# Load slots and look-ahead in a two-layer decoder trunk: eight slots for seven, modulation tiles three ahead for two

## The chip, the core and the metric

The kernel runs on one core of a Trainium2 chip. Its engines are TensorE (PE, with its weight loads PEld in rows of their own), VectorE (DVE), ScalarE (ACT), GpSimd (POOL) and SyncE (SP), which here only issues transfers. Each engine works through its own list of instructions in order. The metric is the device time of one execution in microseconds; lower is better. It is taken as the median of several runs.

## The reference: what is computed

Two decoder layers over one sequence of 256 tokens, width 2048, all in float32. Layer 0 mixes tokens by gated linear attention (GLA), layer 1 by softmax attention with forget gates (FoX); each is followed by a gated MLP of inner width 5632 with a causal convolution of width 3. Every sub-layer is modulated by a vector made from the condition `c`:

```python
cond = jax.nn.silu(c)
for i in range(DEPTH):
    mod = (cond @ w_mod[i] + b_mod[i])[:, None, :]
    sh_m, sc_m, g_m, sh_f, sc_f, g_f = jnp.split(mod, 6, axis=-1)
    h = rmsnorm(x, norm_mix[i]) * (1.0 + sc_m) + sh_m
    y = gla_mixer(h, ...) if i % N_MIXERS == 0 else fox_mixer(h, ...)
    x = x + (1.0 + g_m) * y
    h = rmsnorm(x, norm_ffn[i]) * (1.0 + sc_f) + sh_f
    x = x + (1.0 + g_f) * conv_ffn(h, ffn_w_up[i], ...)
return rmsnorm(x, norm_final)
```

So there are two kinds of large reads. The weights of the mixers and of the MLPs go to TensorE against 256 tokens. The modulation matrix `w_mod` (2 x 2048 x 12288 numbers) meets a single vector, and its product is needed at the start or the end of each sub-layer.

## The kernel before

**Tiles.** Weights come as tiles of 128 x 1024 numbers (4 KB in each of 128 partitions, 512 KB in all). A list made ahead of time, `plan`, holds them in the order of use. The full float32 precision is reached by splitting: ScalarE rounds a weight tile `w` to a high part `wh` (line 117), VectorE computes the rest `wl` (line 121), and TensorE runs three products for each piece (lines 612 to 614; 648 to 650 where the activations are stationary). One weight tile makes 24 matmuls of 128x128 against 256 columns. `wh` and `wl` have `AHEAD + 1` = 4 buffers each, so splits run at most some three tiles ahead of TensorE.

**Modulation.** `w_mod` is read as tiles `wm` of the same size. After the start VectorE takes them: for each one a multiply-add `acc = wm * c + acc` over 128x1024 (line 271, the first of a sum line 269). 16 such tiles make 1024 columns; then `acc` is summed over partitions (lines 283, 284, 300, 304) and written into `mod`. A sub-layer's `h` reads `mod`, and so do the residuals.

**The ring.** `w` and `wm` tiles share one pool of buffers, `ring`, with RING = 7 slots. A transfer into a slot waits until the tile that held it has been read for the last time: a `w` by its split on line 121, a `wm` by its multiply-add. All these transfers stand in SP's one queue, in a fixed order; one that waits for a slot holds up those behind it.

**Who asks when.** `next_w` hands out the next weight tile and calls `split_to`, which issues loads for up to `RING - 1` = 6 tiles ahead of the one to split next. After each tile's matmuls `tick` runs: it calls `prefetch(PEND)`, which issues modulation loads until PEND = 2 of them are pending, and then `steps`, which takes as many multiply-adds from the pending ones (`bg_step`) as `pace["bg"]` says. `set_pace(n)` spreads the queued modulation tiles over n ticks: 32 tiles over 44 ticks in the first GLA stage, over 43 in the first stage of the MLP of layer 0. `drain_bg` takes all that are left, at the ends of such stages.

**What sets the order.** The functions record instructions in the order of the program; a scheduler then orders each engine's list by a timeline of its own, in which it also hands out the slots. `tc.issue_after` keeps a multiply-add behind the latest split. So a change of slots or of load order can shift other instructions by some places.

Of the kernel before, what the change touches and what calls it, by code (L numbers as in the profile page):

```python
# [28 lines left out]
GH = 4  # L29
FH = 16  # L30
SECT = {"sh_m": 0, "sc_m": 1, "g_m": 2, "sh_f": 3, "sc_f": 4, "g_f": 5}
RING = 7
AHEAD = 3
DIRECT = 4
XAFTER = 1
# [2 lines left out]
BACK = 1  # L38
STAGE = 3
FREE = 0  # L40
PEND = 2
BLOCKS = (8, 8)
FIRST = (6, 0)
SLOW = 0.0
# [26 lines left out]
def kernel(  # L71
# [10 lines left out]
    const = ctx.enter_context(tc.tile_pool(name="const", bufs=1))  # L82
    ring = ctx.enter_context(tc.tile_pool(name="ring", bufs=RING))
    big = ctx.enter_context(tc.tile_pool(name="big", bufs=NBIG))
# [15 lines left out]
    def ringt(shape, s="w"):  # L100
        return ring.tile(shape, F32, tag="w", name=nm(s))
# [10 lines left out]
    def split_w(src, moving, after=None):  # L112
        n_ = src.shape[-1]
        o1, o2 = (0, 0) if moving else HELD
        hi = tmp.tile([P, WCOLS], F32R, tag="wh", bufs=AHEAD + 1, name=nm("wh"))[:, o1:o1 + n_]
        lo = tmp.tile([P, WCOLS], F32R, tag="wl", bufs=AHEAD + 1, name=nm("wl"))[:, o2:o2 + n_]
        nc.scalar.copy(out=hi, in_=src)  # L117
        with ExitStack() as es:
            if after is not None:
                es.enter_context(tc.issue_after(after))  # L120
            order["v"] = nc.vector.tensor_tensor(out=lo, in0=src, in1=hi.bitcast(F32), op=ALU.subtract).ins  # L121
        return hi, lo
# [106 lines left out]
    def after_startup(on=True):  # L229
        es = ExitStack()  # L230
        if on and startup["left"] > 0 and len(startup["loads"]) >= BACK:
            startup["left"] -= 1
            es.enter_context(tc.issue_after(startup["loads"][-BACK]))
        return es
# [115 lines left out]
    def prefetch(depth):  # L350
        while bg and len(pending) < depth:
            load, f = bg.popleft()
            load()
            pending.append(f)
# [6 lines left out]
    def flush_resting(all_=False):  # L361

        for r in resting:
            r[0] -= 1
        while resting and (all_ or resting[0][0] <= 0):
            resting.popleft()[1]()

    def tick():
        prefetch(PEND)
        flush_resting()  # L370
        with ExitStack() as es:
            for key in ORDERED:
                if order[key] is not None and fetched["use"] > FREE:
                    es.enter_context(tc.issue_after(order[key]))
            steps()
# [185 lines left out]
    def next_w(kt, cols, hold=None):  # L561
        i = fetched["use"]
        assert plan[i][1] == kt and plan[i][3] == tuple(cols), (plan[i][1:], kt, cols)
        fetched["use"] += 1
        run, look = AHEAD if hold is None else hold, RING - 1
        if i < STAGE:
            run, look = min(run, STAGE - i), 1
        split_to(min(i + 1 + run, len(plan)), look)
        return splits.popleft()

    def split_to(end, look=RING - 1):
        while fetched["split"] < end:
            while fetched["load"] < min(fetched["split"] + look, len(plan)):
                w_, kt_, nk_, cols_, mov_ = plan[fetched["load"]]
                fetched["load"] += 1
                wt = ringt([P, 1024])
                o = 0
                for c0, cn in cols_:
                    if nk_ == 1:
                        with after_startup():  # L580
                            nc.sync.dma_start(out=wt[:, o:o + cn], in_=w_[kt_ * P:(kt_ + 1) * P, c0:c0 + cn])
                        o += cn
                    else:
                        nc.sync.dma_start(out=wt[:, :nk_ * cn].rearrange("p (k r) -> p k r", r=cn),
                                          in_=w_[kt_ * P:(kt_ + nk_) * P, c0:c0 + cn]
                                          .rearrange("(k p) r -> p k r", p=P))
                        nc.vector.memset(wt[:, nk_ * cn:nk_ * cn + P - cn], 0.0)
                        o = nk_ * cn + P - cn
                raws.append((wt[:, :o], mov_))
            with ExitStack() as es:  # L590
                after = None
                if gate["n"] > 0:

                    gate["n"] -= 1
                    es.enter_context(tc.issue_after(gate["early"] if gate["n"] > 0 else gate["late"][0]))
                    after = gate["late"][1]
                splits.append(split_w(*raws.popleft(), after))
            fetched["split"] += 1
# [4 lines left out]
    def stream_a(kts, cols, rhs, done=None):  # L603
# [12 lines left out]
        for k in kts:  # L616
            rh, rl = rhs(k)
            tail = done is not None and k in kts[-TAIL:]
            wh, wl = next_w(k, cols, kts[-1] - k + 1 if tail else None)
            if tail:  # L620
                held.append((k, wh, wl, rh, rl))
                continue
            for m in range(8):
                mms(m, k, wh, wl, rh, rl)
            tick()
        if done is not None:
            split_to(min(fetched["use"] + 1, len(plan)))
            if len(deferred) > 1:
                deferred.pop(0)()
            for m in range(8):  # L630
                for args in held:
                    mms(m, *args)
                if m % 2 == 1:
                    done(m // 2, ps)
        return ps

    def stream_b(kts, c0, lhs):
        ps = [b.rearrange("p j t -> p (j t)") for b in banks()]
        for k in kts:
            lh, ll = lhs(k)  # L640
            wh, wl = next_w(k, [(c0, 1024)])
            first, last = k == kts[0], k == kts[-1]
            for tt in range(TT):
                ts_ = slice(tt * P, (tt + 1) * P)
                for hf in range(2):
                    hs_ = slice(hf * 512, (hf + 1) * 512)
                    o = ps[tt * 2 + hf]
                    nc.tensor.matmul(o, lh[:, ts_], wh[:, hs_], start=first, stop=False)  # L648
                    nc.tensor.matmul(o, ll[:, ts_], wh[:, hs_], start=False, stop=False)  # L649
                    nc.tensor.matmul(o, lh[:, ts_], wl[:, hs_], start=False, stop=last)  # L650
            tick()
        return ps

    def narrow(kts, c0, nn, lhs):
        pa = misc()
        lhs(kts[0])
        nh, nl = next_w(kts[0], [(c0, nn)])
        for k in kts:
            lh, ll = lhs(k)
            cs = slice((k - kts[0]) * nn, (k - kts[0]) * nn + P)  # L660
            first, last = k == kts[0], k == kts[-1]
            nc.tensor.matmul(pa[:, :T], nh[:, cs], lh, start=first, stop=False)
            nc.tensor.matmul(pa[:, :T], nh[:, cs], ll, start=False, stop=False)
            nc.tensor.matmul(pa[:, :T], nl[:, cs], lh, start=False, stop=last)
        return pa
# [669 lines left out]
```

## Time and profile before

| | |
|---|---|
| median of 3 runs | 2452.31 us (2449.97 to 2458.36) |
| the profiled execution | 2452.57 us |
| its span, first to last instruction | 2450.8 us |
| TensorE / VectorE / ScalarE / GpSimd busy | 98% / 79% / 51% / 1% |
| read from HBM | 633.14 MB, 259 GB/s over the span |
| mean granted TensorE clock | 0.987 of full speed |

The span and the busy times come from the first part of the profile. An engine's busy time counts its own instructions; a matmul's end is modelled and overlaps the next one's start, so a busy TensorE can still be held up for parts of a microsecond between two starts, and only a longer hold shows as idle time. A row of the view by stretches of time gives for one stretch its length and, for each engine, the busy time with the number of instructions, then the granted clock, the busy share of the DMA engines and their rate.

### The profile page before, as it was taken

How to read it: one execution, taken by the hardware profiler on the slowest of the kernel's cores; microseconds unless marked ns; L12 is line 12 of the kernel's file. 1: busy time of each engine (PE TensorE's matmuls, PEld its weight loads, DVE VectorE, ACT ScalarE, POOL GpSimd, SP SyncE). 2: the span in 40 equal slices, each digit the busy share in tenths (PEclk: the TensorE clock that was granted, in tenths of full speed). 3: DMA queues.
4: the chain of work that ended last, by engine and by line, in shares of the span. 5: the costliest groups of instructions: out<-in, count | busy, mean ns of one | idle time of the engine just before them, and what ended most of it. 6: DMA issues, size and time to landing. Idle time of an engine off the chain costs nothing.

```text
span 2450.8 us, 46953 instructions
## 1 busy us (share of the span) xinstructions
PE 2401.6 (98%) x19147; PEld 2313.5 (94%) x19150; DVE 1926.7 (79%) x2587; ACT 1254.9 (51%) x1700; POOL 16.5 (1%) x35
## 2 busy tenths in 40 slices
PE   6999999999999999999999999999999999999998
PEld 6998899899999999999988888999999999999998
DVE  7777989887789999987587898887876777777544
ACT  2456555444655555543454545554655555555433
POOL 0000000000000000000000000000000000000000
PEclk7999999899999999999999999999999999999999
DMA  9897878798668888999589887687677777756553
GB/s 371 281 314 239 301 260 313 277 315 313 201 192 273 304 290 307 308 336 320 182 287 311 302 291 235 222 292 250 220 236 233 233 235 237 230 194 220 192 190 112
DMA packets 184309, 638.32 MB, mean 260 GB/s; under 512 B 23961, under 2 KB 24971, under 8 KB 183708
## 3 DMA queue, kind: packets, MB, share of 16 engines
q1 hardware_dynamic: 183128, 634.12, 76.8%
q8 instruction: 150, 2.46, 0.4%
q10 hardware_dynamic: 964, 1.20, 0.1%
q14 instruction: 67, 0.55, 0.1%
HBM read 633.14 MB, written 2.10 MB: 259 GB/s over the span
## 4 chain that ended last, share of the span: by engine, by line
PE 88%; DVE 5%; DMA 5%; issue 1%; ACT 0%; SPq 0%; DVEq 0%; ACTq 0%
PE pa L614 23%; PE pa L613 23%; PE pa L612 23%; PE pa L650 5%; PE pa L649 5%; PE pa L648 5%; DMA wm<-in_w_mod_dram 4%; DVE wl L121 2%; DVE acc L271 1%; PE pm L483 0%; PE pt L293 0%; PE pm L852 0%; DMA w<-in_gla_w_in_dram 0%; PE pm L1063 0%; PE pm L874 0%
## 5 line engine op out<-in xcount | busy, mean ns | idle before, releaser
L117 ACT CAST wh<-w 128x1024 fp32r<-128x1024 f32 x819 | 855.9, 1048 | 985.4 <-PE pa L613 686.2
L121 DVE TENSOR_TENSOR wl<-w,wh 128x1024 fp32r<-128x1024 f32 x819 | 993.4, 1219 | 315.5 <-ACT wh L117 311.3
L613 PE MATMUL pa<-h,wh 128*128 128x256 f32 x3584 | 992.3, 278 | 2.3 <-DVE h L530 2.3
L614 PE MATMUL pa<-h,wl 128*128 128x256 f32 x3584 | 990.8, 278 | 3.5 <-DVE wl L121 3.5
L612 PE MATMUL pa<-h,wh 128*128 128x256 f32 x3584 | 990.6, 278 | 3.3 <-ACT h L528 1.8
L614 PEld LDWEIGHTS pa<-h,wl 128*128 128x128 f32 x3584 | 673.1, 188 | 7.1 <-DVE wl L121 4.5
L613 PEld LDWEIGHTS pa<-h,wh 128*128 128x128 f32 x3584 | 675.5, 189 | 3.3 <-DVE h L530 3.1
L612 PEld LDWEIGHTS pa<-h,wh 128*128 128x128 f32 x3584 | 673.6, 189 | 4.4 <-ACT h L528 2.2
L271 DVE SCALAR_TENSOR_TENSOR acc<-wm,cT,acc 128x1024 f32<-128x1024 f32 x352 | 451.9, 1284 | 131.0 <-DMA wm<-in_w_mod_dram 129.4
L613 PE MATMUL pa<-op,wh 128*128 128x256 f32 x1920 | 527.9, 277 | 0.4 <-DVE op L546 0.4
L612 PE MATMUL pa<-op,wh 128*128 128x256 f32 x1920 | 527.2, 277 | 0.0
L614 PE MATMUL pa<-op,wl 128*128 128x256 f32 x1920 | 523.6, 277 | 0.4 <-DVE wl L121 0.4
L613 PEld LDWEIGHTS pa<-op,wh 128*128 128x128 f32 x1920 | 360.5, 188 | 0.6 <-DVE op L546 0.6
L612 PEld LDWEIGHTS pa<-op,wh 128*128 128x128 f32 x1920 | 359.8, 188 | 0.0
L614 PEld LDWEIGHTS pa<-op,wl 128*128 128x128 f32 x1920 | 357.3, 188 | 0.8 <-DVE wl L121 0.6
L649 PE MATMUL pa<-wh,h 128*128 128x512 f32 x512 | 200.1, 392 | 0.0
L648 PE MATMUL pa<-wh,h 128*128 128x512 f32 x512 | 198.7, 392 | 0.0
L650 PE MATMUL pa<-wl,h 128*128 128x512 f32 x512 | 194.3, 393 | 0.0
L1115 ACT ACTIVATE y<-u,cw 128x256 f32<-128x256 f32 x176 | 101.8, 599 | 30.9 <-DVE act L1131 28.6
L648 PEld LDWEIGHTS pa<-wh,h 128*128 128x128 f32 x512 | 96.2, 188 | 19.3 <-issue 0.2
L650 PEld LDWEIGHTS pa<-wl,h 128*128 128x128 f32 x512 | 95.9, 188 | 19.5 <-DVE wl L121 0.3
L649 PEld LDWEIGHTS pa<-wh,h 128*128 128x128 f32 x512 | 96.2, 188 | 19.1
(258 smaller groups left out, 1350.6 us busy)
## 6 DMA issues: line engine op xcount, KB each, us to landing
wm<-in_w_mod_dram SPq DMA_DIRECT2D x352, 512.0 KB, 5.2
w<-in_ffn_w_up_dram SPq DMA_DIRECT2D x320, 512.0 KB, 4.5
w<-in_ffn_w_down_dram SPq DMA_DIRECT2D x176, 512.0 KB, 4.5
w<-in_fox_w_in_dram SPq DMA_DIRECT2D x128, 512.0 KB, 5.0
w<-in_gla_w_in_dram SPq DMA_DIRECT2D x96, 512.0 KB, 5.1
wm<-in_w_mod_dram SPq DMA_DIRECT2D x16, 1024.0 KB, 12.3
w<-in_gla_w_out_dram SPq DMA_DIRECT2D x32, 512.0 KB, 6.0
w<-in_ffn_w_up_dram SPq DMA_DIRECT2D x64, 256.0 KB, 4.1
```

Of the source, the lines that this page charges most:

```text
L117: nc.scalar.copy(out=hi, in_=src)
L121: order["v"] = nc.vector.tensor_tensor(out=lo, in0=src, in1=hi.bitcast(F32), op=ALU.subtract).ins
L271: nc.vector.scalar_tensor_tensor(out=st["a"], in0=wt[:, j, :], scalar=col, in1=st["a"], op0=ALU.mult, op1=ALU.add)
L612: nc.tensor.matmul(o, wh[:, ms], rh, start=(first and m % 2 == 0), stop=False, skip_group_check=True)
L613: nc.tensor.matmul(o, wh[:, ms], rl, start=False, stop=False, skip_group_check=True)
L614: nc.tensor.matmul(o, wl[:, ms], rh, start=False, stop=last, skip_group_check=True)
L648: nc.tensor.matmul(o, lh[:, ts_], wh[:, hs_], start=first, stop=False)
L649: nc.tensor.matmul(o, ll[:, ts_], wh[:, hs_], start=False, stop=False)
L650: nc.tensor.matmul(o, lh[:, ts_], wl[:, hs_], start=False, stop=last)
L1115: nc.scalar.activation(y, u, AF.Identity, scale=cw[:, l * 3 + 2, r:r + 1], bias=cw[:, 6 + l, r:r + 1])
```

## The change

The ring gets an eighth slot. The look-ahead of the weights, which was tied to the number of slots, gets a constant of its own with the value that it had, 6. The number of modulation tiles that `tick` keeps asked for goes from 2 to 3. The number of multiply-adds per tick, and the tick in which each is recorded, stay as they were.

```diff
-RING = 7
+RING = 8
+LOOK = 6
...
-PEND = 2
+PEND = 3
...
-        run, look = AHEAD if hold is None else hold, RING - 1
+        run, look = AHEAD if hold is None else hold, LOOK
...
-    def split_to(end, look=RING - 1):
+    def split_to(end, look=LOOK):
```

One line is added above, so line 250 of before is line 251 of the changed kernel, and so on.

SP's queue at the end of the first stage of the MLP of layer 0 (`w` are weight tiles, `wm` modulation tiles; numbers only tell tiles apart), before:

```order
L250 DMA wm_6345<-in_w_mod_dram 128x1024
L581 DMA w_6348<-in_ffn_w_up_dram 128x1024
L250 DMA wm_6378<-in_w_mod_dram 128x1024
L581 DMA w_6381<-in_ffn_w_up_dram 128x1024
L250 DMA wm_6411<-in_w_mod_dram 128x1024
L581 DMA w_6422<-in_ffn_w_up_dram 128x1024
L581 DMA w_6453<-in_ffn_w_up_dram 128x1024
L250 DMA wm_6483<-in_w_mod_dram 128x1024
L581 DMA w_6486<-in_ffn_w_up_dram 128x1024
```

The same place of SP's queue now:

```order
L251 DMA wm_6347<-in_w_mod_dram 128x1024
L582 DMA w_6350<-in_ffn_w_up_dram 128x1024
L251 DMA wm_6380<-in_w_mod_dram 128x1024
L582 DMA w_6383<-in_ffn_w_up_dram 128x1024
L251 DMA wm_6413<-in_w_mod_dram 128x1024
L582 DMA w_6424<-in_ffn_w_up_dram 128x1024
L582 DMA w_6455<-in_ffn_w_up_dram 128x1024
L582 DMA w_6486<-in_ffn_w_up_dram 128x1024
```

The two lists end at the same weight tile, `w_6486`. In the first the last modulation tile of the stage (`wm_6483`) stands directly ahead of it; in the second the last one (`wm_6413`) stands three weight tiles ahead of it. The weights keep their order, each with one modulation tile more ahead of it.

VectorE's list where the second GLA stage adds up `q` (the four `L725` rows read the TensorE banks `pa`; `L693` belongs to the gate), before:

```order
L725 TENSOR_TENSOR q_713<-q_713,pa_2007 128x512
L271 SCALAR_TENSOR_TENSOR acc_2078<-wm_2226,cT,acc_2078 128x1024
L725 TENSOR_TENSOR q_713<-q_713,pa_2008 128x512
L121 TENSOR_TENSOR wl_2289<-w_2083,wh_2288 128x1024
L725 TENSOR_TENSOR q_713<-q_713,pa_2009 128x512
L725 TENSOR_TENSOR q_713<-q_713,pa_2010 128x512
```

And now:

```order
L726 TENSOR_TENSOR q_715<-q_715,pa_2007 128x512
L726 TENSOR_TENSOR q_715<-q_715,pa_2008 128x512
L122 TENSOR_TENSOR wl_2291<-w_2085,wh_2290 128x1024
L272 SCALAR_TENSOR_TENSOR acc_2080<-wm_2228,cT,acc_2080 128x1024
L726 TENSOR_TENSOR q_715<-q_715,pa_2009 128x512
L726 TENSOR_TENSOR q_715<-q_715,pa_2010 128x512
```

The multiply-add that stood between the first and the second sum of `q` now stands behind the second one and behind the split that follows it.

## The prediction

> **What bounds the kernel now.** First the busy times, then the chain that ended last:
>
> ```profile
> span 2450.8 us, 46953 instructions
> PE 2401.6 (98%) x19147; PEld 2313.5 (94%) x19150; DVE 1926.7 (79%) x2587; ACT 1254.9 (51%) x1700; POOL 16.5 (1%) x35
> PE 88%; DVE 5%; DMA 5%; issue 1%; ACT 0%; SPq 0%; DVEq 0%; ACTq 0%
> ```
>
> TensorE is the bound: it is busy for 2401.6 of 2450.8 us, so 49.2 us of idle time are all that any change of loads can take away, the start and the end included. The change touches no matmul. The question is which of the 49.2 us lie in the middle and who causes them. The view by stretches of 50 us gives the place (columns: length, busy time of PE, PEld, DVE, ACT, POOL, granted clock, DMA share, GB/s):
>
> ```profile
> 0.00:50.00 50.00, 36.62 (x168) 34.37 (x169) 33.93 (x58) 11.81 (x20) 1.18 (x9) 0.82 0.98 385
> ...
> 150.00:200.00 50.00, 47.21 (x382) 45.69 (x381) 35.36 (x33) 22.37 (x32) 0.00 (x0) 0.99 0.89 302
> 200.00:250.00 50.00, 48.39 (x375) 44.77 (x374) 37.00 (x50) 38.93 (x57) 0.00 (x0) 0.97 0.72 232
> 450.00:500.00 50.00, 45.65 (x335) 42.48 (x335) 41.24 (x68) 21.70 (x29) 0.00 (x0) 0.86 0.70 248
> 500.00:550.00 50.00, 48.79 (x430) 48.59 (x429) 38.85 (x36) 24.87 (x31) 0.00 (x0) 1.00 0.92 323
> 550.00:600.00 50.00, 48.22 (x420) 47.66 (x419) 35.40 (x35) 22.66 (x26) 0.00 (x0) 1.00 0.87 305
> 600.00:650.00 50.00, 47.70 (x417) 47.31 (x417) 38.32 (x57) 27.85 (x37) 0.00 (x0) 1.00 0.73 239
> 650.00:700.00 50.00, 50.00 (x443) 50.00 (x443) 40.76 (x59) 28.64 (x39) 0.00 (x0) 1.00 0.61 194
> 850.00:900.00 50.00, 49.55 (x437) 49.35 (x436) 45.12 (x61) 28.76 (x39) 0.00 (x0) 1.00 0.90 307
> 900.00:950.00 50.00, 49.46 (x433) 49.20 (x433) 47.71 (x64) 28.70 (x42) 0.00 (x0) 1.00 0.90 303
> 950.00:1000.00 50.00, 49.11 (x429) 48.57 (x428) 49.41 (x71) 31.01 (x44) 0.00 (x0) 1.00 0.88 298
> 1000.00:1050.00 50.00, 49.64 (x437) 49.41 (x436) 48.43 (x58) 26.25 (x32) 0.00 (x0) 1.00 0.90 318
> ```
>
> Unhindered, TensorE starts 443 matmuls in 50 us (650 to 700), 0.113 us each, so a weight tile of 24 takes 2.71 us. The other rows fall short of it by 0.4 to 4.4 us. Who is late there tell the lists of waits, of the whole span and of VectorE alone in two stretches (80 to 200, then 500 to 615 us; columns: us in total, times, longest):
>
> ```profile
> ACT wh L117 <- PE pa L613: 686.2, 458, 4.0
> DVE acc L271 <- DMA wm<-in_w_mod_dram: 129.4, 111, 3.2
> ...
> DVE acc L271 <- DMA wm<-in_w_mod_dram: 34.6, 22, 3.2
> ...
> DVE acc L271 <- DMA wm<-in_w_mod_dram: 27.8, 21, 2.6
> ...
> SPq L581 <- DVE wl L121: 958.9, 485, 16.6
> SPq L250 <- DVE wl L121: 304.9, 245, 13.1
> ```
>
> Three things are to be seen. ScalarE's cast of a weight waits mostly for TensorE to free a buffer: weights are there early. VectorE's multiply-add waits for the modulation tile to land, 129.4 us in all. And SP cannot issue a load until a split or a multiply-add has freed a slot. So modulation tiles are late, and weight tiles wait in slots; while VectorE waits, the splits queued behind the multiply-add wait too, and so do the slots that they would free. Mostly the four split buffers cover it. Three places where they do not, in the chain and in VectorE's timeline (start, duration):
>
> ```profile
> 190.66 6.08 DMA wm<-in_w_mod_dram
> 196.84 1.29 DVE acc L271
> 198.18 1.09 PE pm L304 x8
> ...
> 238.95 1.28 DVE L271 SCALAR_TENSOR_TENSOR acc<-wm,cT,acc 128x1024 f32<-128x1024 f32 x1 [1.81 <-DMA wm<-in_w_mod_dram]
> 240.15 0.68 DVE L725 TENSOR_TENSOR q<-q,pa 128x512 f32<-128x512 f32 x1
> ...
> 589.93 6.03 DMA wm<-in_w_mod_dram
> 596.28 0.98 issue
> 597.26 1.50 DVE wl L121 x2
> ```
>
> At 190.66 the last modulation tile of the first GLA stage is issued, lands 6.08 us later, and TensorE's transposes of the sum start only at 198.18. At 238.95 a multiply-add that waited 1.81 us holds up the sum of `q`, whose banks TensorE needs. At 589.93 the late tile holds up a split.
>
> **The change, part by part.** The eighth slot and PEND = 3 belong together. The order of SP's queue shows what they do: every modulation load moves one modulation step forward, and every weight keeps its place with one tile more ahead of it, for which there is one slot more. So a weight waits for the same release as before, and a modulation tile for one that comes a step earlier. A step is 2.71 us over the tiles per tick: 44/32 x 2.71 = 3.73 us in the first GLA stage, 43/32 x 2.71 = 3.64 us in the first MLP stage. The longest waits there are 3.2 and 2.6 us. Each is shorter than a step, so, transfers taking no longer than now, all of them go. What is late next at these places is TensorE itself.
>
> Transfers do take longer when more are under way. At full pace the first MLP stage wants 1 + 32/43 = 1.744 tiles of 0.524 MB in 2.71 us, 338 GB/s. What the DMA engines can do shows the start, 385 GB/s (row above), and this stretch:
>
> ```profile
> 415.00:462.00 47.00, 47.00 (x417) 47.00 (x416) 43.77 (x49) 20.47 (x37) 0.00 (x0) 1.00 0.99 369
> wm<-in_w_mod_dram SPq DMA_DIRECT2D x352, 512.0 KB, 5.2
> ```
>
> 338 is 92% of 369, near the 323 that the stretch from 500 moves today. A landing now takes 5.2 us in the median, 6.03 and 6.08 in the chain's rows; the step less the mean wait of that stretch (27.8/21 = 1.3 us) leaves 2.3 us for longer ones.
>
> The terms, each as idle time of TensorE in the rows above:
> - 150 to 200: 50 - 47.21 = **2.79 us**, the wait at 195. With the last load a step earlier the sum is ready when TensorE gets there: all goes.
> - What follows it (clock in the column before DMA share):
>
> ```profile
> 195.00:199.50 4.50, 1.71 (x16) 1.51 (x15) 2.66 (x4) 1.61 (x5) 0.00 (x0) 1.00 0.74 258
> 199.50:203.00 3.50, 3.50 (x20) 3.50 (x19) 1.38 (x3) 1.86 (x14) 0.00 (x0) 0.51 0.87 267
> 203.00:206.00 3.00, 3.00 (x29) 3.00 (x28) 1.36 (x2) 2.45 (x5) 0.00 (x0) 1.00 0.53 208
> ```
>
> Behind that wait the granted clock is 0.51 for 3.5 us: 3.5 x 0.49 = **1.72 us** lost. Without the wait it should go. It stands at 1.72; its bounds are 0 and 1.72. [...]
> - 200 to 250: **1.61 us**, the wait for `q` at 239. VectorE's list now has the second sum of `q` ahead of that multiply-add, so it no longer depends on the tile: all goes.
> - 500 to 650: 1.21 + 1.78 + 2.30 = **5.29 us**: splits and, at the stage's end near 611, the last sum. The last load is issued three weights earlier. All goes; if the DMA engines give no more than today, nothing does.
> - 850 to 1050: 0.45 + 0.54 + 0.89 + 0.36 = 2.24 us. VectorE is 95 to 99% busy from 900 on, so there its own work is the bound as much as the tiles. I take the first two (0.99) whole and half of the last two (0.62): **1.6 us**; bounds 0.5 and 2.2.
> - 450 to 500: the end of the GLA sub-layer. The 369 GB/s show transfers at their limit, and VectorE's multiply-adds stand ahead of the residual (one now ahead of all its parts, 1.28 us): I take 0. The one tile that is read ahead is worth 0.524 MB / 369 GB/s = 1.4 us, so the bounds are -1.3 and +1.4.
> - At the start of each stage three modulation loads instead of two stand ahead of the next weights. The cover is the weights' lead: casts wait 686.2 us for TensorE, and for weight loads 19.2 us in the stretch where these are latest (row further down). I take 0, bound 1.4 us each.
>
> Sum: 2.79 + 1.72 + 1.61 + 5.29 + 1.6 = 13.0 us. Against the profiled execution's 2452.6 us this gives **2439.6 us**; that execution is 0.3 us above the median, so the same holds for the median.
>
> **The rivals.**
> *The clock at the sub-layer's end.* This row follows the end of the GLA sub-layer:
>
> ```profile
> 467.00:485.00 18.00, 17.76 (x91) 14.98 (x93) 10.59 (x22) 7.51 (x12) 0.00 (x0) 0.66 0.26 92
> ```
>
> 18 x 0.34 = 6.1 us of clock are lost. If the wait ahead of it becomes short enough, this goes too: 2452.6 - 13.0 - 6.1 = 2433.5 us. For it: the tile read ahead. Against: transfers are at 0.99. The wait is most of the 4.35 us that are missing in the row of 450 to 500. [...] Chance 0.10.
>
> *Transfers are the bound.* The waits at single last tiles and the order of `q` improve, but in the long stretches each transfer takes as much longer as it starts earlier. Gain 2.79 + 1.72 + 1.61 = 6.1 us: 2446.5. For it: DMA shares of 0.87 to 0.92 in these rows. Against: 369 GB/s at 0.99. Chance 0.18.
>
> *It does nothing.* The slot is taken, but the waits stay, for instance because the place of a multiply-add moves up as far as its load: 2452.6. SP's and VectorE's lists speak against it. Chance 0.06.
>
> *The weights pay (slower).* From 415 to 462 transfers are at their limit and ScalarE waits for weights there (19.2 us in ten waits):
>
> ```profile
> ACT wh L117 <- DMA w<-in_gla_w_out_dram: 19.2, 10, 3.2
> ```
>
> With a tile more ahead, each weight lands up to 1.4 us later. If the split buffers no longer cover that, the removed waits return as waits for weights, and about six stage starts pay 1.4 us each: 2452.6 + 8.5 = 2461. It decides where a weight's lead falls under 1.4 us. TensorE runs that stretch without a gap now (47.00 of 47), which speaks against it. Chance 0.06.
>
> **How the numbers follow.** Forecast 0.60, clock 0.10, transfers 0.18, nothing 0.06, slower 0.06. A measurement of this kernel can tell about 0.3%, 7.4 us, from no change: 2445 and below is faster, above 2459.7 slower. The forecast (0.58 of its 0.60) and the clock rival make faster: with a little taken off for the spread of the runs shown, 0.66. The rest of the forecast, transfers and nothing make 0.27 for the same; the slower rival with the spread 0.07. The range goes from 2431 (clock rival with the upper bounds) to 2450 (transfers with the lower ones) and leaves out nothing and slower, 0.12, and tails.
>
> **What would show it.** Right: VectorE's waits for modulation tiles in 80 to 200 and 500 to 615 fall from 34.6 and 27.8 us to a few; TensorE's idle time from 500 to 650 goes from 5.29 us to under 1; no halved clock near 200; landings of modulation tiles stay under 8 us. Wrong: these waits shrink but ScalarE's waits for weight loads grow by as much, or landings grow by a whole step, or TensorE's gaps return at the next VectorE instruction.

## The result and the profile after

| | before | after |
|---|---|---|
| median | 2452.86 us (2449.97 to 2458.36, 4 runs) | 2431.65 us (2428.96 to 2432.90, 4 runs) |
| profiled execution | 2452.57 us | 2430.69 us |
| mean granted TensorE clock | 0.987 | 0.991 |

The ratio is 0.9909, with a 95% interval of 0.9890 to 0.9929: about 0.9% faster. The forecast of 2439.6 us had the direction and the mechanism, and took the gain too small by 8 us: 13.0 us were expected, 21.2 came. The median lies at the lower end of the range of 2431 to 2450 us.

First the span, the busy times and the chain's shares of the changed kernel:

```profile
span 2429.0 us, 46930 instructions
PE 2390.3 (98%) x19147; PEld 2307.0 (95%) x19150; DVE 1928.5 (79%) x2587; ACT 1256.3 (52%) x1700; POOL 16.0 (1%) x35
PE 95%; DVE 3%; DMA 1%; issue 1%; ACT 0%; SPq 0%; DVEq 0%
```

TensorE now makes 95% of the chain (88% before), transfers 1% (5% before). Its busy time fell by 11.3 us with the same 19147 matmuls: it had contained short holds between matmuls and stretches at half clock (the mean granted clock rose from 0.987 to 0.991). The waits (whole span, then VectorE alone in 500 to 615 us), the group of multiply-adds and the landing of modulation tiles:

```profile
ACT wh L118 <- PE pa L614: 720.9, 499, 4.9
DVE wl L122 <- ACT wh L118: 410.7, 424, 3.3
...
ACT wh L118 <- DMA w<-in_gla_w_out_dram: 20.5, 11, 3.1
...
DVE wl L122 <- ACT wh L118: 23.3, 34, 1.5
...
L272 DVE SCALAR_TENSOR_TENSOR acc<-wm,cT,acc 128x1024 f32<-128x1024 f32 x352 | 450.2, 1279 | 6.6 <-DMA wm<-in_w_mod_dram 5.8
wm<-in_w_mod_dram SPq DMA_DIRECT2D x352, 512.0 KB, 5.3
```

VectorE's multiply-adds wait 5.8 us for their tiles in the whole span, where they waited 129.4; in 500 to 615 us such a wait is no longer in the list. VectorE now waits for ScalarE's casts, and these wait for TensorE: the work is early everywhere but at TensorE. A tile lands in 5.3 us (5.2 before), and casts wait 20.5 us for the one weight matrix where loads are latest (19.2 before): the transfers did not become slower, and the weights hardly paid.

The view by stretches, same columns as before:

```profile
150.00:200.00 50.00, 50.00 (x416) 48.95 (x415) 34.71 (x32) 25.75 (x45) 0.00 (x0) 1.00 0.89 306
200.00:250.00 50.00, 49.89 (x405) 46.55 (x404) 44.24 (x62) 41.54 (x55) 0.24 (x2) 1.00 0.79 265
450.00:500.00 50.00, 45.30 (x368) 43.80 (x368) 44.01 (x70) 25.05 (x34) 0.00 (x0) 0.97 0.83 271
500.00:550.00 50.00, 50.00 (x443) 50.00 (x442) 40.80 (x42) 23.16 (x27) 0.00 (x0) 1.00 0.95 341
550.00:600.00 50.00, 49.78 (x439) 49.58 (x438) 38.93 (x42) 25.49 (x32) 0.00 (x0) 1.00 0.92 317
600.00:650.00 50.00, 50.00 (x443) 50.00 (x443) 37.15 (x56) 31.61 (x43) 0.00 (x0) 1.00 0.60 189
850.00:900.00 50.00, 50.00 (x443) 50.00 (x442) 48.95 (x72) 29.74 (x40) 0.00 (x0) 1.00 0.88 298
900.00:950.00 50.00, 50.00 (x444) 50.00 (x443) 48.50 (x66) 29.29 (x42) 0.00 (x0) 1.00 0.91 320
950.00:1000.00 50.00, 50.00 (x443) 50.00 (x442) 49.69 (x70) 33.10 (x47) 0.00 (x0) 1.00 0.84 286
1000.00:1050.00 50.00, 50.00 (x443) 50.00 (x443) 44.81 (x46) 20.51 (x21) 0.00 (x0) 1.00 0.96 353
```

From 500 to 550 us TensorE starts 443 matmuls at 341 GB/s, the rate that the prediction worked out as wanted (338). From 950 to 1000 it starts 443 with VectorE busy for 49.69 of 50 us. Most of what is left of loss in the rows shown is in 450 to 500.

**Where the time came from.** Some TensorE instructions stand alone among the matmuls, once at each stage's end, so their start times measure progress better than busy times do. These are the rows of TensorE's timeline for two of them, of before and then of after (start, duration, idle time ahead of it in brackets):

```profile
198.18 1.09 PE L304 MATMUL pm<-ident,acc 128*128 128x128 f32 x8 [2.79 <-DVE acc L271]
...
612.89 0.41 PE L300 MATMUL pm<-red,quad 128*128 128x32 f32 x2 [1.79 <-DVE red L284]
```

```profile
194.11 1.04 PE L305 MATMUL pm<-ident,acc 128*128 128x128 f32 x8
...
594.90 0.30 PE L301 MATMUL pm<-red,quad 128*128 128x32 f32 x2
```

The transposes of the last sum of the first GLA stage start 4.07 us earlier, the sum at the end of the first MLP stage 17.99 us earlier, both without a wait ahead of them. With four more such marks (the mean square at the end of the GLA sub-layer, two more column sums in the MLP of layer 0, and the deferred sum at its end) the span falls into seven sections. Their lengths in us, for the profiled execution of before, for three more executions of the same kernel (below), and for after:

| section, by its end in before | before | again 1 | again 2 | again 3 | after |
|---|---|---|---|---|---|
| start to 198 | 198.18 | 202.63 | 199.36 | 200.76 | 194.11 |
| to 467, end of the GLA sub-layer | 268.72 | 266.41 | 265.07 | 265.42 | 263.21 |
| to 548, into the MLP | 81.16 | 77.81 | 78.51 | 79.28 | 78.16 |
| to 613, its first stage ends | 64.83 | 64.01 | 64.82 | 64.98 | 59.41 |
| to 830 | 217.15 | 217.09 | 218.31 | 217.15 | 216.65 |
| to 1203, the MLP ends | 372.64 | 375.47 | 373.77 | 373.17 | 368.41 |
| the rest, layer 1 | 1248.09 | 1248.10 | 1249.91 | 1248.11 | 1249.01 |

Two things are to be seen. Most of the gain lies in the three sections in which transfers ran at over 300 GB/s before (start to 198 at 320 GB/s, 548 to 613 at 309 and 830 to 1203 at 303; the other four at 234 to 289): 13.7 of 21.8 us in the profiled execution, 16.7 of 21.3 against the mean of the four of before. And the sections of before differ by up to 4.5 us from execution to execution, so a term read from one trace has an error of that size.

The mark at 548 is no clean cut: before, TensorE waits 1.21 us right ahead of it, so that wait of the MLP's first stage counts in the section of the sub-layer's end, and in the changed kernel the mark stands six matmuls later. The terms of the prediction are therefore measured further down between the same matmuls.

### The profile page after: what moved, and what is told of

It is laid out like the page before. It is cut to its first block, busy times and chain, and to the rows that moved or that the text cites. A ratio compares the mean times of both kernels' runs of the same rounds, so it can differ in the third digit from the quotient of the medians.

```text
span 2429.0 us, 46930 instructions
## 1 busy us (share of the span) xinstructions
PE 2390.3 (98%) x19147; PEld 2307.0 (95%) x19150; DVE 1928.5 (79%) x2587; ACT 1256.3 (52%) x1700; POOL 16.0 (1%) x35
## 4 chain that ended last, share of the span: by engine, by line
PE 95%; DVE 3%; DMA 1%; issue 1%; ACT 0%; SPq 0%; DVEq 0%
PE pa L614 25%; PE pa L615 25%; PE pa L613 25%; PE pa L650 5%; PE pa L651 5%; PE pa L649 5%; DMA wm<-in_w_mod_dram 1%; DVE acc L272 1%; DVE wl L122 0%; PE pm L484 0%; PE pm L853 0%; PE pm L875 0%; PE pm L1064 0%; PE pm L1010 0%; PE pm L1028 0%
```

## The experiments

The theory is that the **lead of the modulation tiles** brings the gain: each is asked for one step earlier, and for that the eighth slot, the order, or both may be used. The rival is that **one more load under way** brings it, whichever tile is in it. The first four kernels differ from the changed one in the three numbers alone; one slot more or less, one tile of look-ahead more or less. SP's queue in the trace of slot_only is in the order of before, in that of ask_only in the order of the changed kernel; VectorE's list shifts by places in both.

**slot_only**: the slot alone.

```diff
-PEND = 3
+PEND = 2
```

> Eight slots, modulation tiles two ahead as before, weights six ahead. Theory A (a modulation tile comes a step of some 3.7 us earlier; that lead is the gain): the eighth slot alone brings each load one release earlier, some 1.6 us (2.71 us per 1.74 tiles), against waits of 1.3 us in the mean and up to 3.2 us. So a part of the gain, 5 to 14 of the 21 us: 2438 to 2448 us. Theory B (it is the slot, one load more under way, that gives the gain): all of it, 2430 to 2434 us. Theory C (only the order in the queue counts): nothing, 2450 to 2455 us.

Measured: 2434.14 us (2431.85 to 2436.34); ratio 0.9920 (0.9907 to 0.9933) to 2451.65 us. That is 17.5 us, more than the 5 to 14 that the theory gave for it and close to the rival's range, so this run alone does not tell the two apart. VectorE's wait for modulation tiles, whole span:

```profile
DVE acc L272 <- DMA wm<-in_w_mod_dram: 30.4, 30, 2.7
```

30.4 us in place of 129.4; and SP's waits for a split, before it can issue a modulation tile, fall from 304.9 to 87.9 us. With seven slots, 6 weights ahead and 2 modulation tiles pending want 8 slots, so a load that was due in the order waited for a slot; with eight both fit. So the slot alone, with the old order, gives these tiles most of the lead.

**ask_only**: three pending, seven slots.

```diff
-RING = 8
+RING = 7
```

> Seven slots, modulation tiles three ahead, weights six ahead. Theory A: each modulation load stands a step earlier in SP's queue, each weight has a tile more ahead of it and no slot for it, so weights lose 1.6 us of a lead of 7 us and more; the gain should come nearly whole, 2431 to 2440 us. Theory B: no gain, 2450 to 2455 us. If weights have no lead to give (the slower rival of the prediction), over 2455 us, with casts that wait for weight loads.

Measured: 2437.61 us (2435.90 to 2439.75); ratio 0.9936 (0.9924 to 0.9948). Without any new slot 14.0 us come from the order alone. What it costs stands in the waits of the whole span:

```profile
ACT wh L118 <- DMA w<-in_gla_w_out_dram: 25.2, 14, 3.4
ACT wh L118 <- DMA w<-in_ffn_w_down_dram: 17.7, 10, 2.6
...
DVE acc L272 <- DMA wm<-in_w_mod_dram: 11.3, 15, 2.4
```

The multiply-adds wait 11.3 us, and the casts wait longer for weights (19.2 and 10.2 us for these two matrices before): the lead was taken from these. It hurts in one place. The section that ends with the GLA sub-layer takes 269.93 us, against 263.21 in the changed kernel and 265.07 to 268.72 in the four executions of before; a half clock of 3.41 us at 226.49 lies in it too. So the prediction's rival in which the weights pay is seen in part, with the old seven slots.

**look_five**: the changed kernel, with the eight slots and the three pending, and the weights five ahead.

```diff
-LOOK = 6
+LOOK = 5
```

> Eight slots, modulation tiles three ahead, weights five ahead. Theory A with weights that have lead to spare: as the change or up to 3 us faster, 2428 to 2434 us. If the weights' lead is what carries the stretch from 415 to 455 us, where casts wait for weight loads, slower there by some us: 2435 us and more.

Measured: 2433.64 us (2431.81 to 2434.83); ratio 0.9920 (0.9907 to 0.9933). The weights have nearly a tile of lead to spare: with one less, casts wait 27.4 us for the matrix at the GLA sub-layer's end, and the time stays within some 2 us of the changed kernel's.

**slot_weights**: eight slots, the new one given to a weight.

```diff
-LOOK = 6
+LOOK = 7
...
-PEND = 3
+PEND = 2
```

> Eight slots, modulation tiles two ahead, weights seven ahead: the slot goes to a weight. Theory A: a modulation load then has a slot more and a weight more ahead of it, which cancel: 2448 to 2456 us, VectorE's waits for modulation tiles as before (129 us in all). Theory B: one load more under way whatever it is, 2430 to 2436 us.

Measured: 2451.48 us (2443.78 to 2457.31); ratio 0.9994 (0.9982 to 1.0006).

```profile
DVE acc L272 <- DMA wm<-in_w_mod_dram: 127.9, 115, 4.2
```

As many slots as in slot_only, and nothing gained: the multiply-adds wait 127.9 us, as before (the trace is that of its fastest execution, 2443.78 us). The rival falls. What counts is which tile has the lead.

**The sub-layer's end.** In the profiled executions the same matmuls take 3.8 us less across the end of the GLA sub-layer after the change (460 to 500 us of before), and this is a part that the forecast had at nothing. The chain of waits there, before:

```profile
466.89 4.64 PE pm L483 x10
471.53 3.20 PE pt L293 x16
474.73 0.24 issue
474.98 3.19 PE pm L518 x7
```

and after:

```profile
456.84 0.44 DVE ss L477
457.32 2.43 PE pm L484 x10
459.75 1.68 PE pt L294 x16
461.50 1.67 PE pm L519 x7
```

The same three groups of TensorE take 11.3 us from start to end before (466.89 to 478.17) and 5.9 us after (457.32 to 463.17): before, they stand in 13.65 us of half clock that begin at 465.74. TensorE's idle time ahead of them is 3.90 us before and 2.42 us after. Is it the longer wait that brings the half clock? Filler matmuls on TensorE in that wait shorten it without touching a load. They are recorded after the last matmul of the sub-layer, ahead of the mean square's; VectorE's, ScalarE's and SyncE's lists stay as in the kernel before. The lines that set `gap` and `order["m"]` are left out here:

```diff
+                if gap["n"] and m == 5:
+                    continue
+                if gap["n"] and m == 7:
+                    with tc.issue_after(order["m"]):
+                        pw = misc()
+                        for _ in range(gap["n"]):
+                            nc.tensor.matmul(pw, fill[:, :P], fill, start=True, stop=True)
+                    done(2, ps)
                 if m % 2 == 1:
                     done(m // 2, ps)
...
```

**before_fill12**, with gap["n"] = 12 on the kernel before:

> The kernel before, with 12 filler products of 512 columns (about 0.24 us each, 2.9 us) on TensorE in its wait at the end of the GLA sub-layer (4.06 us between two starts, followed by 13.65 us at half clock). Theory, the length of this wait brings the half clock, which costs 6.0 us: the wait falls to about 1.2 us, no half clock behind it, 2446.9 us. Rival, the half clock comes from something else, and the 6 us that the changed kernel gained there came from its earlier loads: half clock stays, 2452.9 us.

Measured: 2447.43 us (2442.05 to 2450.64, 12 runs), against 2451.98 us; ratio 0.9985 (0.9973 to 0.9996), so 3.7 us, between 1.0 and 6.6. In its timeline (11 of the 12 fillers in this row):

```profile
463.24 2.54 PE L640 MATMUL pm<-fill 128*128 128x512 bf16 x11
466.52 0.70 PE L484 MATMUL pm<-ss,onesD 128*128 128x256 f32 x2 [0.74 <-DVE ss L477]
```

The idle time is 0.74 us and no half clock follows. Filling the wait does gain; the 6.0 us that the one trace of before suggested lie inside the interval, near its end. One trace without a half clock does not yet show that the wait brings it.

**before_fill4**, the same with 4:

> The same with 4 filler products (about 1 us), so that about 3.1 us of the wait remain, near the 2.77 us that eight slots alone left there without a half clock. Theory, the length of the wait decides: no half clock, 2446.9 us, if 3.1 us are short enough, and 13.65 us of half clock and 2452.9 us, if not. Rival as above: 2452.9 us.

Measured: 2450.61 us (2445.66 to 2459.54, 12 runs); ratio 1.0001 (0.9987 to 1.0015). Its profiled execution has 2.48 us of idle time there, no half clock, and took 2445.66 us, the fastest of the twelve; the median did not move. So that one trace is no proof that a shorter wait keeps the half clock away. This one is inconclusive, and it asked for the next three.

**before_again1, before_again2, before_again3**: the kernel before, unchanged.

> The kernel before, unchanged, profiled again. Its executions lie between 2441 and 2458 us. Theory, the same wait at the end of the GLA sub-layer (4 us) is followed by a half clock in one execution and not in another, and that makes most of the spread: where an execution takes 2452 us or more its trace has some 10 us or more of half clock between 190 and 620 us beside the wait, where it takes 2447 us or less it has 7 us or less. Rival, the half clock of 13.65 us is there every time and the spread comes from transfers.

> As the first of the three: by theory the time follows the half clock between 190 and 620 us, half a microsecond for each, by the rival it does not.

> As the first of the three: by theory the time follows the half clock between 190 and 620 us, half a microsecond for each, by the rival it does not.

Measured: 2453.23, 2451.55 and 2450.58 us. The half clock behind the wait at the sub-layer's end lasts 0, 3.41 and 3.41 us, where the first trace had 13.65: it is not there every time, which refutes the rival as it was put. But the theory fails too. The slowest of the three has no half clock at all between 190 and 620 us. Its first section is the longest of the four, 202.63 us, and there it waited for modulation tiles, as its timeline and VectorE's waits from 80 to 200 us show:

```profile
202.63 1.09 PE L304 MATMUL pm<-ident,acc 128*128 128x128 f32 x8 [3.65 <-DVE acc L271]
...
DVE acc L271 <- DMA wm<-in_w_mod_dram: 35.9, 21, 5.7
```

The longest wait for a tile is 5.7 us here and was 3.2 in the first trace, and TensorE waits 3.65 us in place of 2.79 for the last one. So two sources of the spread of the kernel before are seen: how late the tiles land, and where a half clock falls. That they make up all of it, 2440.77 to 2457.00 us in the runs beside these experiments, is not shown: the four profiled executions lie within 2.7 us.

**after_fill4**: the changed kernel, with gap["n"] = 4.

> The changed kernel with 4 filler products at the same place, where it waits 2.58 us with no half clock behind. Theory: nothing there to remove, 2431.7 us, within 1.5 us. Rival, filler work before the new stage itself makes the clock better later on: the half clock of 3.41 us at 473.6 goes too, 2430.0 us.

Measured: 2431.85 us (2429.06 to 2436.13, 6 runs). Nothing was gained there; the half clock at 473.45 stays.

**after_late**: the changed kernel, whose first multiply-add of the MLP's first stage is put off.

```diff
-    set_pace(8 * FIRST[0] - N5)
+    set_pace(8 * FIRST[0] - N5 - 2)
+    pace["acc"] = -1.0
```

> The changed kernel, where the first multiply-add of the first MLP stage of layer 0 is recorded about one tick later and the pace is raised so that the 32 still end in the stage. In the changed kernel it stands ahead of a part of h, for which TensorE waits 2.20 us at 469.6, with a half clock of 3.41 us (1.7 us lost) behind it; by the products after it some 3.0 us of the gain are given back there. Theory, that multiply-add (0.67 us) is part of the new wait: the wait falls to about 1.5 us, the half clock goes, 2431.7 - 0.7 - 1.7 = 2429.3 us; if the half clock stays, 2431.0 us. Rival, the lead that the delay costs comes due at the end of the stage near 600 us: 2433 us or more.

Measured: 2430.89 us (2430.38 to 2432.02, 6 runs). The wait for `h` in the changed kernel, and then in this one:

```profile
472.08 0.39 PE L614 MATMUL pa<-h,wh 128*128 128x256 f32 x1 [2.20 <-DVE h L531]
```

```profile
473.93 0.38 PE L614 MATMUL pa<-h,wh 128*128 128x256 f32 x1 [1.55 <-DVE h L531]
```

It falls by 0.65 us, about the duration of the multiply-add, and no half clock follows; the section to 548 takes 75.21 us in place of 78.16, of which six matmuls fewer ahead of the mark are 0.7 us. In this execution the gain is given back elsewhere: the section to 467, with a half clock at 226.05, takes 265.08 in place of 263.21 us, the first one 194.74 in place of 194.11, and the two from 548 to 830 together 276.74 in place of 276.06. By the times it can't be told from the changed kernel, and none of these runs beats that one.

## Why the prediction fell short, step by step

The sum, term by term. A term is measured between two matmuls of the main products: both kernels start 18048 of them, into the banks `pa`. Counted in order, the gain of a stretch is the time from its first matmul to its last before, less the time between the matmuls with the same numbers after. The third column is the profiled execution, the fourth the mean of the four executions of before, each against the one profiled execution of after:

| term, by its stretch before | taken | profiled execution | mean of four |
|---|---|---|---|
| start to 190 | 0 | 1.11 | 3.15 |
| wait at 195 and half clock at 200 (190 to 205) | 2.79 + 1.72 | 4.64 | 3.42 |
| `q` (205 to 245) | 1.61 | 1.99 | 1.27 |
| 245 to 460 | 0 | 0.35 | 0.45 |
| the sub-layer's end (460 to 500) | 0 | 3.79 | 0.77 |
| 500 to 650 | 5.29 | 6.61 | 7.29 |
| 650 to 850 | 0 | 0.00 | 0.05 |
| 850 to 1050 (to 1060) | 1.6 | 4.23 | 5.33 |
| the rest, with layer 1 | 0 | -0.92 | -0.46 |
| sum | 13.0 | 21.8 | 21.3 |

**The mechanism held.** Modulation loads came a step earlier and the waits shorter than a step went: 129.4 us of waits became 5.8, and landings stayed at 5.3 us. No half clock is left near 200, and TensorE idles for 0.22 us from 500 to 650. In slot_weights, where these tiles are as late as before, nothing is gained in the median. One thing was wrong in it: the slot and the order do not need each other, for either alone brings most of the gain (17.5 and 14.0 us).

**The step that failed is that losses were read as idle time of TensorE.** The prediction opens with it: 49.2 us of idle time are all that any change of loads can take away. The span fell by 21.8 us, and only 10.5 of them are idle time (49.2 to 38.7 us); the other 11.3 came out of busy time, where half clock and short holds between starts had been. A modelled matmul end hides holds of parts of a microsecond (in the rows of before a matmul into `pa` lasts 0.28 us, and the next starts after 0.11), as the reading note on the profile said, and I did not apply it. The starts in the same rows held a better measure, and two terms show it. They hold 4.0 of the 8.8 us that are missing in the third column, and 5.7 of 8.3 in the fourth.

*850 to 1050* was mis-sized twice. I took TensorE's idle time, 2.24 us, as all that there was, and then only 1.6 of it. The rows count 437 + 433 + 429 + 437 = 1736 starts, where 4 x 443 = 1772 fit. 36 starts of 0.113 us are 4.1 us, and 4.23 came. And the reason for taking the last two rows half, that VectorE at 95 to 99% was a bound of its own there, is refuted by the row 950 to 1000 of after: VectorE is busy for 49.69 us and TensorE loses nothing. Its busy share had no bearing while its results came in time.

*500 to 650* was taken at its idle time of 5.29 us. Its rows count 430 + 420 + 417 = 1267 starts before and 443 + 439 + 443 = 1325 after: 58 starts more, 6.6 us, and 6.61 came between the same matmuls.

**The start to 198 was read from a favourable execution.** The last tile's wait of 2.79 us went, as said. The first 88 us differed too, by 0.9 us: the half clock of the start lasted 34.13 in place of 37.55 us, which again 1 of the unchanged kernel has as well, with the same 0.9 us at 88 us. That is no work of the change. The other executions of before took 1.2 to 4.5 us more for this section; in all three TensorE also waits for the first sum near 136 us (2.14, 1.26 and 1.03 us), which the first trace does not show. The changed kernel has no such waits to vary: look_five, slot_only and after_fill4 reach the mark at 194.12, 194.18 and 193.96.

**The half clock at 200 (1.72)** was there and went, in that execution. In the three others of before it was not there, so against the mean the row falls short of 4.51; in the traces of before_fill12 and before_fill4, which are the kernel before up to this place, it is there (at 200.88 and 199.77). Three of six have it, so in the median it is worth less than it was taken for.

**The sub-layer's end, taken as 0**, is the step that failed in kind. The wait there became 1.48 us shorter in the profiled execution (3.90 to 2.42), about the upper bound of 1.4 that I kept for the tile read ahead, and the half clock behind it went; that transfers ran at 369 GB/s with a DMA share of 0.99, which the prediction took for their limit, was the argument for 0 and did not keep the wait from shrinking. The clock rival (2433.5 us) named the next effect, and its time came nearest, but partly by luck: the half clock that it would remove is 13.65 us long in one execution of four and 0 or 3.41 in the others, filling the wait gains 3.7 us (1.0 to 6.6) in the median, and most of what the forecast lacked came from the other rows. In exchange a wait of 2.20 us for `h` appears in the new stage, 0.65 us of it the multiply-add, with 3.41 us of half clock behind it. Against the mean 0.77 us stay.

What shortened the wait is open. It goes with the slot and not with the lead of the modulation tiles: without fillers it is 2.17 to 2.77 us in the five kernels with eight slots, slot_weights among them with 2.17, and 3.13 to 3.91 us in the four executions of before and in ask_only. A half clock follows it in four of these last five traces and in none of the first five. How often it does in all executions of the old kernel, and so what its going is worth in the median, is left open as well: the four executions are too few, and before_fill4 did not move the time.

**Other rivals.** "Transfers are the bound" is refuted by the 341 GB/s at full pace; "it does nothing" by the waits; "the weights pay" is seen in part in ask_only, where no slot pays for the lead, in the one stretch named.

## What to carry to other kernels

When loads of two kinds share slots and a queue, ask whose lead is short, and give the slot to that one: the same slot was worth 17.5 us to the tiles that were late and nothing that the times show to those that were early. Size a loss at a busy engine by the instructions that it started against its best row, not by idle time: 36 missing starts were 4.1 us where 2.24 us were idle, and in the profiled execution half of the whole gain came out of busy time. And read a term of a few microseconds from several executions before it is taken for the kernel's: between executions of one kernel the sections here differed by up to 4.5 us.

## What the runs showed of the hardware

In all thirteen profiled executions the granted clock changes on a grid: the stretches of half clock within one execution begin whole multiples of 3.4133 us apart (before: 199.50, 465.74 and 2442.05 us, 78.00 and 579.00 steps; after: 33.31, 473.63 and 2422.64 us, 129.00 and 571.00 steps), and those in the middle last one step (3.41 us) or four (13.65 us). What followed a wait went in these traces with where it lay on the grid, and not with its length alone. The view by stretches, first of before for the two grid steps that meet at 199.50, and then of before_again1 for two stretches in which TensorE is wholly idle, each with the one behind it:

```profile
196.09:199.50 3.41, 1.32 (x12) 1.33 (x13) 2.66 (x4) 0.82 (x5) 0.00 (x0) 1.00 0.70 234
199.50:202.91 3.41, 3.41 (x19) 3.41 (x18) 1.38 (x3) 1.86 (x14) 0.00 (x0) 0.50 0.88 270
```

```profile
199.00:202.40 3.40, 0.00 (x0) 0.00 (x0) 1.11 (x1) 0.95 (x1) 0.00 (x0) 1.00 0.67 270
202.60:206.00 3.40, 3.37 (x30) 3.37 (x31) 2.71 (x4) 2.43 (x16) 0.00 (x0) 1.00 0.66 206
465.60:469.00 3.40, 0.00 (x0) 0.00 (x0) 3.35 (x8) 2.55 (x5) 0.00 (x0) 1.00 1.08 267
469.00:472.40 3.40, 3.36 (x21) 3.11 (x21) 0.39 (x1) 0.90 (x2) 0.00 (x0) 1.00 0.40 121
```

In before the step with 1.32 us of work was followed by one at a clock of 0.50; in before_again1 two stretches of 3.40 idle microseconds, each across two steps of its grid, were followed by a clock of 1.00.

Over the thirteen traces, from 85 to 2400 us, TensorE's busy time in a step at full clock nearly tells which steps are followed by a half clock. All 13 with 0.20 to 1.45 us are. Of those with 1.58 us or more only three are. Between them one with 1.55 us is (470.22 us in after), and two with 1.50 and 1.51 us are not. The three lie between 222 and 230 us in ask_only, slot_weights and after_late and are busy throughout; what brings the half clock behind them is not shown. So in these traces some 1.9 us of idle time inside one step (3.41 less 1.45 to 1.55) were enough, and 3.40 us across two steps were twice followed by none. How short a wait must be, which the clock rival of the prediction left open, is no matter of length alone here: the wait of 2.20 us for `h` in the changed kernel is followed by a half clock, that of 3.65 us in before_again1 is not.

The second is the spread. The kernel before ran from 2440.77 to 2457.00 us in one set of 23 runs, over 16.2 us; beside it, after_late and after_fill4, which hardly wait for tiles, stayed within 1.6 and 7.1 us, though in six runs each.
